# A two-layer decoder trunk: FFN features split ahead, attention values by key tile, HGRN2 scores in half columns, one fill tile moved

## The chip, the cores and the metric

One core of a Trainium2 chip runs the whole program, compiled as one launch. The metric is the device time of one execution in microseconds (us); the times of a kernel are the median of several executions.

## What is computed

The reference is a trunk of two layers over 512 tokens of 1024 features, in float32. Each layer runs a half-step SwiGLU feed-forward network (FFN), three token mixers beside each other on one normalised input, and a second FFN; every part has an RMS norm before and after.

```python
y = swiglu(rms_norm(h, ffn1_pre_g[l]), ffn1_w_gate[l], ffn1_w_up[l], ffn1_w_down[l])   # (silu(x @ gate) * (x @ up)) @ down
h = h + 0.5 * rms_norm(y, ffn1_post_g[l])
u = rms_norm(h, mix_pre_g[l]);  proj = u @ w_in[l]
y_a = rwkv7_branch(...)      # 8 heads x 64
y_b = mla_branch(...)        # 8 heads, causal softmax attention, values of 64
y_c = hgrn2_branch(...)      # 4 heads x 128, gated linear recurrence in chunks of 64
merged = gates[0] * (y_a @ rwkv_out[l]) + gates[1] * (y_b @ mla_out[l]) + gates[2] * (y_c @ hgrn_out[l])
h = h + rms_norm(merged @ w_o[l], mix_post_g[l])
# and FFN 2 like FFN 1
```

Inside a chunk of 64 tokens, HGRN2 needs the causal scores between all pairs of tokens of the chunk, each with its own product of decays. In MLA each head has softmax(q k) over the earlier keys, times its values.

## The kernel before

**Precision.** The dense products are done in three: an operand is split into a high half in the fp32r format (a cast on ScalarE, ACT, line L208) and the rest (a subtraction on VectorE, DVE, L209), and TensorE (PE) multiplies high by high, high by low and low by high (L251 to L253). Weights of 128 x 1024 or so arrive in `ws` (two buffers) through the DMA queue of SyncE (SP), and become `wh` and `wl` (three buffers each). Small products (scores, transposes) are plain float32, which PE runs in two recorded passes per instruction.

**Order of the work.** The code says which products there are; a list scheduler then lays out one queue per engine, so the order on an engine isn't that of the code. Temporary tiles `t` (seven buffers) and `m` (four), the big slots `s0` to `s10`, and the eight PSUM banks `b0` to `b7` limit how far work can be pulled ahead. The HGRN2 scores and the MLA scores take their PSUM tiles from three banks (`"a"`).

**FFN.** `gate_up` makes the inner features `hid` (22 tiles of 128 features by 512 tokens). All blocks of 256 features but the first two are done by `seven`, a seven-product scheme on half matrices; its last product ends in a SiLU (L1189) and a multiplication (L1190). `down` then multiplies the tiles of `hid` with the down weights into all eight banks. Its operand for tile j comes from the function `chunk` in `ffn`, which takes two `t` tiles, `hh` and `hl`, and splits `hid` tile j into them.

**Mixers.** `mixers` runs RWKV, then `hgrn`, then `mla`. A generator yields 41 fill tiles, projections of 24 matmuls each with 512 columns, which `pump` inserts at named places: the table `PUMP` gives how many at each (`C0` and `C1` are in `hgrn`, `B0` and `B1` in `mla`), and what is left of the 41 follows `mla`. Behind it come the output projections of the three branches.

**HGRN2 scores.** For four heads and the levels `base`, 32, 16 and 8, `hgrn` computes scores between scaled keys and queries and puts them together in `acc`. At `base`, 16 and 8 the function `scores` multiplies whole tiles of 128 x 128 tokens (L737, four per head), and a `copy_predicated` of 128 x 512 per head (L753) takes over what a mask allows; only pairs within one chunk of 64 tokens are ever taken. Level 32 has its own products of 32 x 32 (L776) and copies (L778). Behind level 8 stands `pump("C1")`, and then the keys `kx` (L783 to L785) and their transposes.

**MLA.** For each head, four row blocks: scores (L1032), row maximum, exp (L1038), scaling (L1040), transposes of the probabilities by PE (L204), a copy of them to `pT` (L1044). After each odd head the values of both heads of the pair are multiplied with `pT` into one bank, head e into partitions 64e to 64e + 63, by row block b and then key tile j (L1053, 128 columns each).

## Time and profile before

| | us |
|---|---|
| median of three runs | 2741.38 (2739.57 to 2741.49) |
| the profiled execution | 2739.44 |
| its span, first to last instruction | 2737.7 |
| PE busy | 2682.2 (98% of the span) |
| PE weight loads, beside the matmuls | 2337.6 (85%) |
| DVE busy | 1773.6 (65%) |
| ACT busy | 1348.2 (49%) |
| mean granted clock of PE | 0.994 of 2.4 GHz |

The page is read from the top: which engine is busy nearly all the time, then what that engine waited for and where, then the timeline at those places. A matmul's recorded duration includes the time it takes to run out of the array, so what a matmul costs PE is the distance from its start to the next start. A float32 matmul has two records.

### The profile page before, as it was taken

What the parts mean: (1) busy time and instruction counts of PE and PEld (TensorE: products, weight loads), DVE (VectorE), ACT (ScalarE), POOL (GpSimd) and SP (SyncE); (2) the same over time, 40 slices, a digit from 0 to 9 for tenths busy, and PEclk for the clock granted to TensorE, in tenths of its full rate; (3) what the DMA queues carried; (4) which work ended last, traced back from release to release, by engine and by line L of the source; (5) the groups of instructions that cost most, each with busy time, mean ns of one, the idle gap of its engine ahead of it and who ended that gap; (6) DMA issues with size and microseconds to landing.
All of it is one profiled execution on the core that took longest, in us unless ns stands there. A gap on an engine that the chain in (4) does not pass through costs nothing. (4 is left out here: it accounts for less than half of the span.)

```text
span 2737.7 us, 42564 instructions
## 1 busy us (share of the span) xinstructions
PE 2682.2 (98%) x17669; PEld 2337.6 (85%) x17669; DVE 1773.6 (65%) x2483; ACT 1348.2 (49%) x2133; POOL 58.7 (2%) x121
## 2 busy tenths in 40 slices
PE   8999999989999999999999999999899999999999
PEld 7998887777887889998899988877678878899987
DVE  6786357864856667784468754477558566678743
ACT  4444346346658544443344443464465585444532
POOL 0000010000000010000000000100000000100000
PEclk9999999999999999999999999999999999999999
DMA  4333332325321541333313333233253315322332
GB/s 142 110 107 123 117 123 85 112 86 173 128 86 63 172 172 62 121 105 114 123 57 98 104 127 125 99 105 101 74 204 101 106 63 180 139 93 93 116 108 77
DMA packets 223517, 307.71 MB, mean 112 GB/s; under 512 B 11856, under 2 KB 181052, under 8 KB 221788
## 3 DMA queue, kind: packets, MB, share of 16 engines
q1 hardware_dynamic: 223324, 304.99, 33.3%
q8 instruction: 139, 2.28, 0.3%
q14 instruction: 54, 0.44, 0.0%
HBM read 269.84 MB, written 35.13 MB: 111 GB/s over the span
## 5 line engine op out<-in xcount | busy, mean ns | idle before, releaser
L253 PE MATMUL b<-xhi,wl 128*128 128x256 f32 (+1 forms) x2176 | 733.5, 337 | 0.0
L251 PE MATMUL b<-xhi,wh 128*128 128x256 f32 (+1 forms) x2176 | 733.4, 337 | 0.0
L252 PE MATMUL b<-xlo,wh 128*128 128x256 f32 (+1 forms) x2176 | 732.1, 336 | 0.0
L208 ACT CAST wh<-ws 128x1024 fp32r<-128x1024 f32 (+4 forms) x448 | 393.7, 890 | 660.9 <-PE b L252 296.8
L209 DVE TENSOR_TENSOR wl<-ws,wh 128x1024 fp32r<-128x1024 f32 (+4 forms) x448 | 453.5, 1022 | 266.0 <-ACT wh L208 261.2
L251 PEld LDWEIGHTS b<-xhi,wh 128*128 128x128 f32 x2176 | 414.4, 190 | 45.1 <-issue 4.9
L253 PEld LDWEIGHTS b<-xhi,wl 128*128 128x128 f32 x2176 | 414.4, 190 | 42.0 <-issue 2.8
L252 PEld LDWEIGHTS b<-xlo,wh 128*128 128x128 f32 x2176 | 414.7, 191 | 40.6 <-issue 2.6
L251 PE MATMUL b<-s,wh 128*128 128x256 f32 (+1 forms) x1120 | 344.6, 308 | 0.0
L252 PE MATMUL b<-s,wh 128*128 128x256 f32 (+1 forms) x1120 | 344.2, 307 | 0.0
L253 PE MATMUL b<-s,wl 128*128 128x256 f32 (+1 forms) x1120 | 344.1, 307 | 0.0
L208 ACT CAST wh<-m 128x1024 fp32r<-128x1024 f32 x144 | 151.1, 1049 | 232.2 <-PE b L252 99.5
L251 PE MATMUL b<-wh,t 128*128 128x512 f32 x576 | 225.3, 391 | 8.1 <-ACT t L208 8.1
L252 PE MATMUL b<-wl,t 128*128 128x512 f32 x576 | 224.7, 390 | 0.0
L251 PEld LDWEIGHTS b<-s,wh 128*128 128x128 f32 x1120 | 213.9, 191 | 11.0 <-DVE s L994 1.2
L253 PE MATMUL b<-wh,t 128*128 128x512 f32 x576 | 223.3, 390 | 0.0
L253 PEld LDWEIGHTS b<-s,wl 128*128 128x128 f32 x1120 | 213.9, 191 | 10.0
L252 PEld LDWEIGHTS b<-s,wh 128*128 128x128 f32 x1120 | 214.0, 191 | 9.7
L209 DVE TENSOR_TENSOR wl<-m,wh 128x1024 fp32r<-128x1024 f32 x144 | 174.0, 1223 | 34.7 <-ACT wh L208 34.7
L209 DVE TENSOR_TENSOR t<-s,t 128x512 fp32r<-128x512 f32 x80 | 54.9, 691 | 166.5 <-PE b L252 150.3
L251 PEld LDWEIGHTS b<-wh,t 128*128 128x128 f32 x576 | 108.4, 188 | 31.4 <-ACT t L208 8.9
L252 PEld LDWEIGHTS b<-wl,t 128*128 128x128 f32 x576 | 108.5, 188 | 22.6
(328 smaller groups left out, 4005.6 us busy)
## 6 DMA issues: line engine op xcount, KB each, us to landing
ws<-in_w_in_dram SPq DMA_DIRECT2D x58, 1024.0 KB
ws<-in_ffn_w_up_dram SPq DMA_DIRECT2D x44, 1024.0 KB
ws<-in_ffn_w_down_dram SPq DMA_DIRECT2D x44, 1024.0 KB
ws<-in_ffn_w_gate_dram SPq DMA_DIRECT2D x43, 1024.0 KB
gd<-f SPq DMA_DIRECT2D x48, 256.0 KB
t<-gd SPq DMA_DIRECT2D x48, 256.0 KB
s<-cd SPq DMA_DIRECT2D x8, 1024.0 KB
ws<-in_w_o_dram SPq DMA_DIRECT2D x8, 1024.0 KB
```

Source lines behind the costliest of these rows:

```text
L208: self.nc.scalar.copy(hi, src)
L209: self.nc.vector.tensor_sub(lo, src, hi.bitcast(F32))
L251: nc.tensor.matmul(out, whi, xhi, start=start, stop=False, **kw)
L252: nc.tensor.matmul(out, whi, xlo, start=False, stop=False, **kw)
L253: nc.tensor.matmul(out, wlo, xhi, start=False, stop=stop, **kw)
```

## The change

Four edits.

1. *FFN.* The split of `hid` tile 0 is called in `gate_up` ahead of the last `seven`, and `down` uses that result for j = 0. `chunk` gets `hid` as an argument.
2. *HGRN2 scores.* Per token tile of 128 two products of 64 x 64 (one per chunk, u = 0 and 1, on the two column halves of the array) stand in place of one of 128 x 128; two `copy_predicated` of 64 x (4 x 64) per head stand in place of one of 128 x 512.
3. *MLA values.* The loops go by key tile j first, and each product takes all later query columns: 512, 384, 256 and 128, for both heads in turn. 8 instructions per head pair stand in place of 20.
4. *Fill.* `C1` of the table goes from 0 to 1: one fill tile of 24 matmuls comes behind the level 8 scores and no longer behind `mla`.

```diff
-    "C0": (1, 0, 1), "C1": 0, "C2": 0, "C3": 0, "B": 5, "B0": (0, 1, 0, 0), "B1": (0, 0, 0, 0, 1, 0, 0, 0),
+    "C0": (1, 0, 1), "C1": 1, "C2": 0, "C3": 0, "B": 5, "B0": (0, 1, 0, 0), "B1": (0, 0, 0, 0, 1, 0, 0, 0),
...
-        def scores(lhs, rhs, merge):
+        U = [slice(0, 64), slice(64, 128)]
+        def scores(lhs, rhs, mask):
+            mk = self.c(mask).bitcast(I32)
             for h in range(4):
-                ps = self.psum("a", (P, NT, P))
+                ps = self.psum("a", (P, NT, CH))
                 for t in range(NT):
-                    tk = slice(t * P, (t + 1) * P)
-                    nc.tensor.matmul(ps[:, t, :], lhs[:, h, tk], rhs[:, h, tk], start=True, stop=True)
-                merge(h, ps)
+                    for u in range(2):
+                        tk = slice(t * P + u * CH, t * P + u * CH + CH)
+                        nc.tensor.matmul(ps[U[u], t, :], lhs[:, h, tk], rhs[:, h, tk], start=True, stop=True)
+                for u in range(2):
+                    nc.vector.copy_predicated(acc[U[u], h, :, U[u]], mk[U[u], U[u]].unsqueeze(1).broadcast_to([CH, NT, CH]), ps[U[u]])
...
-                for b in range(NT):
-                    tk = slice(b * P, (b + 1) * P)
-                    for j in range(b + 1):
-                        for e in range(2):
-                            g = h - 1 + e
-                            nc.tensor.matmul(o[N[e], tk], vn[:, j, 64 * g:64 * g + 64], pTs[e][:, j, tk], start=j == 0, stop=j == b)
+                for j in range(NT):
+                    tk = slice(j * P, T)
+                    for e in range(2):
+                        g = h - 1 + e
+                        nc.tensor.matmul(o[N[e], tk], vn[:, j, 64 * g:64 * g + 64], pTs[e][:, j, tk], start=j == 0, stop=j == NT - 1)
...
                     A = self.token_sums()
+                if c == FF // 256 - 1:
+                    self.begun = chunk(hid, 0, -1)
                 self.seven(A, self.load(wg, KD, 256, col0=c * 256), self.load(wu, KD, 256, col0=c * 256),
...
-        self.down(NF, self.a[f"ffn{n}_w_down"][l], chunk, (0, 1, 2, 5), done)
+        self.down(NF, self.a[f"ffn{n}_w_down"][l], lambda j, n: chunk(hid, j, n) if j else self.begun, (0, 1, 2, 5), done)
```

How the queues change, at three places. In a row, `b` is a PSUM bank's tile, `s` a slot, `<-` stands between what is written and what is read, and x4 joins four alike. After the change the lines are numbered higher by 2 to 5.

PE at the boundary of the last FFN, before; `xhi`, `wl` are the last gate/up product, `t_24022` the high half of `hid` tile 0:

```order
L253 MATMUL b_3487_23790<-xhi_92,wl_23980 128x256
L251 MATMUL b_3512_24012<-wh_24026,t_24022 128x512
L252 MATMUL b_3512_24012<-wl_24027,t_24022 128x512
L251 MATMUL b_3513_24013<-wh_24026,t_24022 128x512
L252 MATMUL b_3513_24013<-wl_24027,t_24022 128x512
L251 MATMUL b_3514_24014<-wh_24026,t_24022 128x512
L252 MATMUL b_3514_24014<-wl_24027,t_24022 128x512
L251 MATMUL b_3515_24015<-wh_24026,t_24022 128x512
```

PE at the same boundary, after; `t_23809` and `t_23810` are the halves of `hid` tile 0, and L251 with `b_3515` is the first to write the bank of the last SiLU:

```order
L253 MATMUL b_3489_23818<-xhi_92,wl_24008 128x256
L251 MATMUL b_3514_24040<-wh_24050,t_23809 128x512
L252 MATMUL b_3514_24040<-wl_24051,t_23809 128x512
L253 MATMUL b_3514_24040<-wh_24050,t_23810 128x512
L251 MATMUL b_3516_24042<-wh_24050,t_23809 128x512
L252 MATMUL b_3516_24042<-wl_24051,t_23809 128x512
L253 MATMUL b_3516_24042<-wh_24050,t_23810 128x512
L251 MATMUL b_3517_24043<-wh_24050,t_23809 128x512
L251 MATMUL b_3515_24041<-wh_24050,t_23809 128x512
L252 MATMUL b_3515_24041<-wl_24051,t_23809 128x512
```

The down matmuls of the first bank read `t_24022`, cast behind the last SiLU, before, and `t_23809` after; the bank of that SiLU is first written by the eighth matmul after. ACT at this boundary, before, the SiLU (L1189) and behind it the cast of `hid` tile 0:

```order
L208 CAST wh_24026<-ws_24020 128x1024
L208 CAST wh_24058<-ws_24020 128x1024
L208 CAST wh_24092<-ws_24086 128x1024
L1189 ACTIVATE t_24007<-b_3487_23790 128x512
L208 CAST t_24022<-s_3236_21643 128x512
```

ACT after, two pieces: where the cast of `hid` tile 0 now stands, behind the SiLU of the block before, and the last SiLU (now L1194) with the cast of tile 1:

```order
L1194 ACTIVATE t_23806<-b_3460_23589 128x512
L208 CAST t_23809<-s_3236_21667 128x512
L208 CAST wh_23917<-ws_23813 128x1024
L1170 COPY t_23853<-b_3489_23818 128x512
L208 CAST wh_23947<-m_23851 128x1024
```

```order
L208 CAST wh_24050<-ws_24048 128x1024
L208 CAST wh_24082<-ws_24048 128x1024
L208 CAST wh_24116<-ws_24110 128x1024
L1194 ACTIVATE t_24035<-b_3489_23818 128x512
L208 CAST t_24078<-s_3236_21667 128x512
```

The cast moved from behind the last SiLU to 13 rows ahead of it. PE at the `base` scores of layer 0, before (L251 and L252 are fill matmuls, the L252 row the first of 23):

```order
L216 MATMUL b_931_6555<-t_6557,ones_3759 128x512
L737 MATMUL b_937_6587<-s_935_6573,s_936_6574 128x128 x4
L251 MATMUL b_944_6621<-xhi_92,wh_6617 128x512
L737 MATMUL b_938_6593<-s_935_6573,s_936_6574 128x128 x4
L737 MATMUL b_939_6599<-s_935_6573,s_936_6574 128x128 x4
L737 MATMUL b_940_6605<-s_935_6573,s_936_6574 128x128 x4
L252 MATMUL b_944_6621<-xlo_93,wh_6617 128x512
```

PE there, after (the L251 row at the end is the first of 21 fill matmuls):

```order
L216 MATMUL b_931_6555<-t_6557,ones_3759 128x512
L742 MATMUL b_937_6587<-s_935_6573,s_936_6574 64x64 x8
L251 MATMUL b_944_6641<-xhi_92,wh_6637 128x512
L252 MATMUL b_944_6641<-xlo_93,wh_6637 128x512
L253 MATMUL b_944_6641<-xhi_92,wl_6638 128x512
L742 MATMUL b_938_6598<-s_935_6573,s_936_6574 64x64 x8
L742 MATMUL b_939_6609<-s_935_6573,s_936_6574 64x64 x8
L742 MATMUL b_940_6620<-s_935_6573,s_936_6574 64x64 x8
L251 MATMUL b_944_6641<-xhi_92,wh_6637 128x512
```

Two fill matmuls moved from behind the scores of heads 1 to 3 to ahead of them. DVE there, before: merges of the four heads, other work of MLA's norms (L967), two subtractions of level 16, copies of level 32 (L778):

```order
L753 COPY_PREDICATED s_934_6571<-consts_64,b_937_6587 128x512
L753 COPY_PREDICATED s_934_6571<-consts_64,b_938_6593 128x512
L967 SCALAR_TENSOR_TENSOR m_6528<-m_6528,vt_3753,t_6539 128x512 x2
L967 SCALAR_TENSOR_TENSOR m_6529<-m_6529,vt_3753,t_6539 128x512
L967 SCALAR_TENSOR_TENSOR m_6529<-m_6529,vt_3753,t_6552 128x512
L967 SCALAR_TENSOR_TENSOR m_6530<-m_6530,vt_3753,t_6552 128x512
L753 COPY_PREDICATED s_934_6571<-consts_64,b_939_6599 128x512
L753 COPY_PREDICATED s_934_6571<-consts_64,b_940_6605 128x512
L762 TENSOR_TENSOR s_950_6693<-s_914_6502 128x64x16
L763 TENSOR_TENSOR s_950_6693<-s_914_6502 128x64x16
L778 COPY s_934_6571<-b_946_6649 32x4x32 x2
```

DVE there, after (merges L744, norms L969, subtraction L764, copies L780):

```order
L744 COPY_PREDICATED s_934_6571<-consts_64,b_937_6587 64x4x64 x2
L744 COPY_PREDICATED s_934_6571<-consts_64,b_938_6598 64x4x64
L969 SCALAR_TENSOR_TENSOR m_6528<-m_6528,vt_3753,t_6539 128x512 x2
L969 SCALAR_TENSOR_TENSOR m_6529<-m_6529,vt_3753,t_6539 128x512
L969 SCALAR_TENSOR_TENSOR m_6529<-m_6529,vt_3753,t_6552 128x512
L969 SCALAR_TENSOR_TENSOR m_6530<-m_6530,vt_3753,t_6552 128x512
L744 COPY_PREDICATED s_934_6571<-consts_64,b_938_6598 64x4x64
L744 COPY_PREDICATED s_934_6571<-consts_64,b_939_6609 64x4x64 x2
L744 COPY_PREDICATED s_934_6571<-consts_64,b_940_6620 64x4x64 x2
L764 TENSOR_TENSOR s_950_6713<-s_914_6502 128x64x16
L780 COPY s_934_6571<-b_946_6669 32x4x32 x2
```

Each merge became two, one half of head 1 stands ahead of the norms, and one of the two subtractions moved behind the copies. PE among the first MLA heads of layer 0, before; L204 are transposes of probabilities, L1032 and L1034 scores of the next head:

```order
L204 MATMUL b_1108_7629<-consts_64,t_7625 128x128 x2
L1053 MATMUL b_1115_7666<-s_1098_7597,s_1037_7206 64x128
L1053 MATMUL b_1115_7666<-s_1081_7528,s_1037_7206 64x128
L1032 MATMUL b_1124_7709<-m_7690,m_7689 128x256
L1034 LDWEIGHTS ident_656_4672
L1034 MATMUL b_1124_7709<-causal_657_4673,ident_656_4672 128x128
L1032 MATMUL b_1124_7709<-m_7690,m_7689 128x256
L1053 MATMUL b_1115_7666<-s_1098_7597,s_1037_7206 64x128
L1053 MATMUL b_1115_7666<-s_1081_7528,s_1037_7206 64x128
L204 MATMUL b_1111_7644<-consts_64,t_7640 128x128 x3
```

PE after, at the end of the first head pair (scores are L1034 and L1036):

```order
L204 MATMUL b_1119_7754<-consts_64,t_7750 128x128 x4
L1036 LDWEIGHTS ident_656_4672
L1036 MATMUL b_1135_7822<-causal_657_4673,ident_656_4672 128x128
L1034 MATMUL b_1135_7822<-m_7772,m_7771 128x512 x2
L1034 MATMUL b_1143_7848<-s_1039_7296,s_1037_7294 128x128
L1055 MATMUL b_1120_7760<-s_1103_7691,s_1041_7298 64x512
L1055 MATMUL b_1120_7760<-s_1086_7622,s_1041_7298 64x384
L1055 MATMUL b_1120_7760<-s_1103_7691,s_1041_7298 64x384
L1055 MATMUL b_1120_7760<-s_1086_7622,s_1041_7298 64x256
L1055 MATMUL b_1120_7760<-s_1103_7691,s_1041_7298 64x256
L1055 MATMUL b_1120_7760<-s_1086_7622,s_1041_7298 64x128
L1055 MATMUL b_1120_7760<-s_1103_7691,s_1041_7298 64x128
```

The value products, single pairs between transposes and scores before, stand in one group of seven behind the last transposes of the pair; an eighth (64 x 512 of the even head) stands alone 18 rows ahead of it. On PE, 43 fill matmuls follow the last value product of a layer before the change, and 11 after it; ahead of the kx transposes there are 33 more.

## Rows read from the trace of the kernel before

**Rows 1.** The page, part 1: busy us, share of the span, instructions.

```profile
PE 2682.2 (98%) x17669; PEld 2337.6 (85%) x17669; DVE 1773.6 (65%) x2483; ACT 1348.2 (49%) x2133; POOL 58.7 (2%) x121
```

**Rows 2.** PE's waits: line, what it waited for: us, times, longest.

```profile
PE b L251 <- ACT t L208: 8.1, 4, 2.0
...
PE b L737 <- ACT t L961: 2.7, 2, 1.4
```

**Rows 3.** Last FFN boundary, timeline: start, us, engine, line, tiles, count [idle <- releaser].

```profile
2609.00 0.28 PE L253 MATMUL b<-xhi,wl 128*128 128x256 f32 x1
...
2609.20 1.04 ACT L208 CAST wh<-ws 128x1024 fp32r<-128x1024 f32 x1 [1.78 <-PE b L252]
2610.16 0.59 ACT L1189 ACTIVATE t<-b 128x512 f32<-128x512 f32 x1
...
2610.64 1.13 ACT L208 CAST t<-s 128x512 fp32r<-128x512 f32 x2
...
2611.30 0.50 PE L251 MATMUL b<-wh,t 128*128 128x512 f32 x1 [2.02 <-ACT t L208]
```

**Rows 4.** Windows, first FFN boundary: length, busy by engine (PE first), PEclk, DMA.

```profile
248.00:250.00 2.00, 2.00 (x7) 1.52 (x6) 2.00 (x5) 1.96 (x4) 0.00 (x0) 0.50 0.57 231
250.00:252.00 2.00, 2.00 (x8) 1.65 (x7) 1.02 (x2) 0.22 (x1) 0.00 (x0) 0.72 0.00 0
```

**Rows 5.** Timeline of PE, layer 0, scores of levels base and 32.

```profile
729.09 2.94 PE L737 MATMUL b<-s,s 128*128 128x128 f32 x24 [1.36 <-ACT t L961]
731.79 0.47 PE L252 MATMUL b<-xlo,wh 128*128 128x512 f32 x1
...
739.13 0.45 PE L776 MATMUL b<-s 128*32 128x32 f32 x16 [0.53 <-DVE s L778]
```

**Rows 6.** Timeline of PE, RWKV part of layer 0, products of 64 columns.

```profile
607.75 0.40 PE L253 MATMUL b<-xhi,wl 128*128 128x512 f32 x1
607.98 0.39 PE L251 MATMUL b<-xhi,wh 128*128 128x512 f32 x1
608.30 0.69 PE L597 MATMUL b<-t,s 128*64 128x64 f32 x16
608.82 0.64 PE L609 MATMUL b<-s,t 128*64 128x64 f32 x16
609.38 0.50 PE L252 MATMUL b<-xlo,wh 128*128 128x512 f32 x1
```

**Rows 7.** Timeline of DVE, layer 0, merges and copies of the scores.

```profile
734.90 1.38 DVE L753 COPY_PREDICATED s<-consts,b 128x512 f32<-128x512 int32 x2
736.14 1.23 DVE L762 TENSOR_TENSOR s<-s 128x1024 f32<-128x1024 f32 x1
...
738.41 1.80 DVE L778 COPY s<-b 32x128 f32<-32x128 f32 x6
```

**Rows 8.** Window, line L1053 alone, layer 0 (PE, PEld); timeline of PE.

```profile
840.00:905.00 65.00, 14.51 (x160) 9.08 (x160) 1.00 0.22 70
...
855.86 0.66 PE L1053 MATMUL b<-s,s 128*64 128x128 f32 x8
856.44 0.66 PE L204 MATMUL b<-consts,t 128*128 128x128 f32 x4
857.03 0.44 PE L1053 MATMUL b<-s,s 128*64 128x128 f32 x4
857.40 0.68 PE L1032 MATMUL b<-m,m 128*128 128x384 f32 x2
```

**Rows 9.** A window in the heads of MLA, layer 0, all engines.

```profile
862.00:876.00 14.00, 14.00 (x106) 10.43 (x105) 11.13 (x39) 12.64 (x35) 0.00 (x0) 1.00 0.17 58
```

**Rows 10.** Timeline of DVE behind the last attention values, layer 0.

```profile
899.07 5.70 DVE L209 TENSOR_TENSOR s<-s,s 128x512 fp32r<-128x512 f32 x9 [3.20 <-PE b L1053]
```

**Rows 11.** Lines L1038 (exp), L1044 (copy): ns min/median/max, first, last start, forms.

```profile
L1038 ACT ACTIVATE t<-b,mx x64: 367/554/707, 834.2 to 2254.0; 128x128 f32<-128x128 f32 x16, 128x256 f32<-128x256 f32 x16, 128x384 f32<-128x384 f32 x16, 128x512 f32<-128x512 f32 x16
...
L1044 ACT COPY s<-b x64: 264/432/588, 842.5 to 2257.1; 128x128 f32<-128x128 f32 x16, 128x256 f32<-128x256 f32 x16, 128x384 f32<-128x384 f32 x16, 128x512 f32<-128x512 f32 x16
```

More of the change, by code (lines that the diff above doesn't have):

```diff
@@ L749, in hgrn @@
         next(norms)
-        def merge(name):
-            mk = self.c(name).bitcast(I32).unsqueeze(1).broadcast_to([P, NT, P])
-            return lambda h, ps: nc.vector.copy_predicated(acc[:, h], mk, ps)
-        scores(xk, xq, merge("base"))
+        scores(xk, xq, "base")
         for i, n in enumerate((32, 16, 8)):
@@ L768, in hgrn @@
             if n < 32:
-                scores(xs, xs, merge(f"lv{n}"))
+                scores(xs, xs, f"lv{n}")
                 continue
@@ L1067, with gate_up @@
 class Trunk(Rwkv, Hgrn, Mla, Core):
-    def gate_up(self, l, n):
+    def gate_up(self, l, n, chunk):
         nc = self.nc
@@ L1243, in ffn, with chunk @@
         nc = self.nc
-        hid = self.gate_up(l, n)
-        g = self.bcast_gain(self.a[f"ffn{n}_post_g"][l])
-        if n == 1:
-            gn = self.bcast_gain(self.a["mix_pre_g"][l])
-        elif not last:
-            gn = self.bcast_gain(self.a["ffn1_pre_g"][l + 1])
         late = []
-        def chunk(j, n):
+        def chunk(hid, j, n):
             if n < 0:
@@ L1261, in chunk @@
             return hh, hl
+        hid = self.gate_up(l, n, chunk)
+        g = self.bcast_gain(self.a[f"ffn{n}_post_g"][l])
+        if n == 1:
+            gn = self.bcast_gain(self.a["mix_pre_g"][l])
+        elif not last:
+            gn = self.bcast_gain(self.a["ffn1_pre_g"][l + 1])
         def done(t, y):
```

## Prediction

> **What bounds the kernel now.** I read the page's busy shares first, then the list of what TensorE (PE) waited for, then the timeline around each wait that the change can reach. PE is busy 98% of the span [rows 1], so time is won only by taking PE work away or closing a PE wait. Two entries of the list of waits lie where the change works [rows 2]: 8.1 us in four pieces, the start of each feed-forward (FFN) down product, and 2.7 us in two, the HGRN2 scores. The sum below is made against the profiled execution (2739.44 us) and taken off the median of the runs, 2741.38; the 1.9 us between them is part of the uncertainty.
>
> **Part 1, FFN.** At the last boundary the final gate/up matmul starts at 2609.00 and the first down matmul at 2611.30. In between ScalarE (ACT) casts a weight, applies a SiLU (L1189, from 2610.16, 0.59) and only then casts the first features, t at 2610.64, for which PE stood idle 2.02 us [rows 3]. The change puts that cast and its subtraction into the previous block, so the first down matmul waits only for weights, and the six behind it write banks that are long free. What is late next is a PSUM bank: the eighth down matmul writes the bank that the SiLU reads. It arrives at 2609.12 + 7 x 0.23 = 2610.7, the SiLU ends at 2610.75, so 0 to 0.1 us stays here; in the first FFN the tenth is gated, which is later still. Gain 2.0 each, 8.0 for four. The moved cast (0.57, half of the pair at 2610.64) goes to an engine that stands idle in every product of that block (the weight cast at 2609.20 had waited 1.78 for PE [rows 3]), its subtraction to DVE, which waits there as well, so they cost nothing; without that cover each would cost about its 0.6.
> The first boundary holds more. After its 2.0 us of idle the granted clock is 0.50 in the stretch 248 to 250, half of 2.4 GHz, and 0.72 in the next [rows 4]: (1 - 0.50) x 2 + (1 - 0.72) x 2 = 1.6 us of work lost. The other three boundaries show no such fall. PE was fully busy before the wait and nothing else differs, so without the idle I expect no fall. FFN: 9.6, bounds 2.2 (below, third rival) and 9.7.
>
> **Part 2, scores.** Before, 96 matmul records a layer of 128 columns: 24 of them take 729.09 to 731.79, 0.1125 each [rows 5], so 10.8 us. After, twice as many instructions of 64 x 64, alternately on the two column halves of the array. The nearest row is L597, the same alternation with 64 columns: 16 records from 608.30 to 608.82, 0.52 us; entering that layout costs 0.32 - 0.23 = 0.09 and leaving it 0.56 - 0.52 = 0.04 [rows 6]. Twelve heads x 0.52 + six clusters x 0.13 = 7.0, gross gain 3.8 a layer.
> These entries and exits are new here, since the old scores used the whole array like their neighbours. The Trainium skill, TensorEngine Tiling (Array Packing), section Key Properties, has it that changing the tiling mode drains TensorE; that speaks against cutting work into small clusters. The rows agree, at 0.13 us a cluster, and the sum without this price would be 0.8 us a layer better.
> Two waits change the 3.8. First, PE waits 1.36 for ACT's logarithms at 729.09 [rows 5]; that time is set by ACT and stays, but three fill matmuls stand ahead of the wait instead of one, so 2 x 0.23 = 0.46 more is done by then. Second, VectorE (DVE). At 734.90 it starts its last two merges (1.38 for two, 0.69 each), then two subtractions (736.14 to 738.41), then the copies for which PE waited until 739.13 [rows 5, 7]. After, five half merges and one subtraction stand ahead of those copies. No row shows a half merge: a copy of 128 columns takes 0.30, a merge of 512 columns 0.69 [rows 7]; 256 columns by a straight line between them are 0.43. So the copies begin at 734.90 + 5 x 0.43 + 1.13 = 738.2 and PE goes on at 738.9: 0.23 + 0.46 = 0.7 ahead of before, where its own work would have put it 1.4 ahead. The two later levels each gain 32 x 0.1125 - 4 x 0.52 - 0.26 = 1.26, as 13 to 31 fills stand between them and DVE. Sum 0.7 + 2.5 = 3.2, and 3.9 if a half merge costs 0.30; I take 3.3, so 6.6 for both layers, bounds -2.4 (second rival) and 7.9.
>
> **Part 3, attention values.** Before, 160 records a layer cost 14.5 us of PE [rows 8], which counts records while they overlap; by starts it is a little more. Eight records last 855.86 to 856.44, 0.58, and four 857.03 to 857.40, 0.37 [rows 8]. So four more records, one key tile of both heads, cost 0.21, and a cluster 0.16 besides, with the entry 0.24. The 22 clusters of a layer hold 48 such steps (40, and eight more where a head stands alone): 48 x 0.21 + 22 x 0.24 = 15.4. After there are two clusters per head pair instead of five or six: one lone matmul of 512 columns and a group of seven (512, 384, 384, 256, 256, 128, 128, the heads in turn). If the two column halves run beside each other at unequal widths as they do at equal ones, the second head's 1280 columns set the group: 10 x 0.21 + 0.24 = 2.34; the lone one costs 4 x 0.21 + 0.24 = 1.08. Four pairs x 3.42 = 13.7, with the 0.21 rounded up 14.1; I take 13.9. The group also waits for the last copy of transposed probabilities, 0.59 [rows 11], which starts when the transposes end; a few score matmuls stand between, so I put under 0.1 a pair, 0.3 a layer. Gain 15.4 - 13.9 - 0.3 = 1.2 a layer, 2.4 in all; bounds -8.0 (first rival) and 3.4.
>
> **Part 4, the fill tile.** 24 matmuls move from the end of MLA to behind the last scores; PE's work is unchanged: 0. There they cover the subtraction, exp and product that end in the kx transposes and are now queued on DVE behind eight half merges; PE, which the scores release sooner, would otherwise wait there. The price is the cover at the end: 11 fill matmuls, 2.5 us, instead of 43, 9.8 us, stand between the last attention values and the output projections. DVE's low halves begin when the last value matmul releases their slot, nine in 5.70 us [rows 10], 0.63 each; even if the first begins 1 us behind that matmul it is done at 1.6, PE wants it at 2.5 and each next one 0.7 later. 0.9 is left; the weight split has already gone by. The stores of the gate tiles and the loads of the next weights on the DMA queue come a tile earlier or later, against 24 x 0.23 = 5.5 us of slack a tile. 0, bounds 0 and -2 (a late first low half, 1 us a layer).
>
> **Sum.** 9.6 + 6.6 + 2.4 = 18.6; 2741.4 - 18.6 = **2722.8 us**, 0.7% faster.
>
> **Rivals.** First, *unequal widths don't overlap*: the 768 columns of the other head in each group then stand in line: 6 x 0.21 = 1.3 more per pair, 10.4 in all, attention loses 8.0 instead of winning 2.4: 2733.2. For it: no row has two widths side by side. Against: four more records cost 0.21 [rows 8], where four of the full array take 4 x 0.1125 = 0.45 [rows 5], so each half goes on by itself.
> Second, *the merges bound the scores*: a half merge costs as much as a whole one, 0.69. Then the copies at level 32 come at 734.90 + 3.45 + 1.13 = 739.5, 1.1 later than before, and the eight merges of each later level take 5.5 us of DVE between scores: I walk to 1.2 lost per layer instead of 3.3 won, 2731.8. Against: the 0.30 copy [rows 7]. The Trainium skill states this rule in TensorEngine Tiling (Array Packing), section PSUM Bottleneck: tiling speeds up the matmuls but not the reading out of PSUM. No run here shows yet which it is.
> Third, *the split ahead doesn't reach PE*: some bank or slot holds the first down matmul until the SiLU's end at 2610.75. Then each boundary wins 2611.30 - 2610.75 = 0.55, 2.2 in all, perhaps with the clock fall left: 2730.2. Against: in the new order the bank of that SiLU comes eighth.
> Fourth, the slow side, *a softmax chain laid open*: the old small value clusters stood in PE's row between scores and transposes, and so bridged the way through exp, transposes and copy, 0.71 + 0.66 + 0.59 = 2.0 us for the widest block [rows 8, 11] (its scaling apart). With values gathered in one group the bridge goes. Open once in each of 16 heads that is 32 us: 2741.4 - 16.2 + 32 = 2757. It decides the sign from (16.2 + 5.5) / 16 = 1.4 us a head. For it: ACT is busy 12.64 of 14 us there [rows 9], so it has little to give. Against: eight more fills now stand between the heads, 1.8 us a layer, and PE was busy 14.00 of 14.00 us there [rows 9].
>
> **How the numbers follow.** A measurement here can tell about 0.2%, 5.5 us, from no change, so "faster" is below 2735.9. Forecast 0.60, first rival 0.13, second 0.09, third 0.07, fourth 0.04; 0.07 for partial losses that add up to within 0.2% (new short waits, a clock fall somewhere else). Faster 0.88, same 0.07, slower 0.05. All upper bounds together give 2741.4 - 9.7 - 7.9 - 3.4 = 2720, less the 1.9 by which single executions differ, 2718; the first rival with its spread gives 2734. The range 2718 to 2734 leaves out some 0.15.
>
> **What would show it.** After the change: the entry "L251 <- ACT t" of four times 2.0 gone from PE's list of waits, and clock 1.00 throughout 246 to 254; score records of about 32 ns and half merges near 0.43; the copies behind the fills still waited for by PE for about 1 us a layer; the group of seven lasting 2.4 us (3.7 if the first rival holds); no wait of PE at the kx transposes or at the first output projection; PE idle within MLA under 1 us a layer (fourth rival if above 10). A PE that waits in MLA would break the forecast most.

## The result

| | before | after |
|---|---|---|
| median, us | 2742.94 (2739.29 to 2746.99, 12 runs) | 2726.2 (2724.63 to 2736.5, 12 runs) |
| ratio | | 0.9947, 95% interval 0.9935 to 0.9959 |
| profiled execution, us | 2739.44 | 2736.01 |

The change makes the kernel 0.5% faster: by the ratio 14.5 us (11 to 18), by the medians of the runs made together 16.7. The forecast was 2722.8, with a range from 2718 to 2734. The profiled execution of after is 10 us above its own median, because for 25 us in RWKV of layer 0 its granted clock was at the lower level (shown at the end; only kernels with the split ahead show it); so the two profiles are compared by stretches and not by their spans.

The page of after, part 1, against [rows 1]: PE still has 98%, and VectorE (DVE) has 6 us more work.

```profile
PE 2683.8 (98%) x17669; PEld 2331.5 (85%) x17669; DVE 1779.8 (65%) x2507; ACT 1347.4 (49%) x2133; POOL 58.5 (2%) x121
```

PE's waits in after, those that the change touches, against [rows 2] (us, times, longest):

```profile
PE b L742 <- ACT t L963: 2.0, 2, 1.0
...
PE b L778 <- DVE s L744: 1.8, 4, 0.5
...
PE b L251 <- DVE s L996: 1.3, 2, 0.7
PE b L778 <- DVE s L780: 1.1, 2, 0.6
...
PE b L742 <- DVE s L768: 0.5, 2, 0.3
PE b L204 <- DVE s L787: 0.4, 2, 0.2
```

The entry of 8.1 us at the FFN boundaries is gone. New are small entries that name DVE: half merges (L744), products of the scores and of kx (L768, L787), and a product in MLA's query projections (L996) that the change does not touch. The one of 1.1 us at level 32 (L780) was there before.

**The FFN boundary in after**, against [rows 3]: timeline of PE, then of ACT, at the last FFN.

```profile
2607.71 0.28 PE L253 MATMUL b<-xhi,wl 128*128 128x256 f32 x1
2607.83 0.40 PE L251 MATMUL b<-wh,t 128*128 128x512 f32 x1
```

```profile
2588.75 0.59 ACT L1194 ACTIVATE t<-b 128x512 f32<-128x512 f32 x1
2589.24 0.61 ACT L208 CAST t<-s 128x512 fp32r<-128x512 f32 x1
...
2607.91 1.05 ACT L208 CAST wh<-ws 128x1024 fp32r<-128x1024 f32 x1 [1.77 <-PE b L252]
```

The cast of `hid` tile 0 is at 2589.24, 18 us ahead of the boundary, and the first down matmul starts 0.12 us behind the last gate/up matmul (before 2.30). At the first boundary the clock stays up, where [rows 4] has 0.50 and 0.72. Windows of after (length, busy by engine with PE first, granted clock, DMA):

```profile
248.00:250.00 2.00, 2.00 (x10) 1.65 (x10) 2.00 (x5) 1.63 (x4) 0.00 (x0) 1.00 0.97 399
250.00:252.00 2.00, 2.00 (x11) 1.65 (x10) 1.85 (x3) 1.02 (x2) 0.00 (x0) 1.00 0.03 8
```

**The scores in after**, against [rows 5]: PE in layer 0, levels base, 32 and 16.

```profile
734.76 0.69 PE L742 MATMUL b<-s,s 128*64 128x64 f32 x16
...
737.32 1.73 PE L742 MATMUL b<-s,s 128*64 128x64 f32 x48 [0.98 <-ACT t L963]
...
744.81 0.45 PE L778 MATMUL b<-s 128*32 128x32 f32 x16 [0.40 <-DVE s L744]
...
745.75 0.45 PE L778 MATMUL b<-s 128*32 128x32 f32 x16 [0.50 <-DVE s L744]
...
747.64 0.45 PE L778 MATMUL b<-s 128*32 128x32 f32 x16 [0.55 <-DVE s L780]
```

```profile
754.95 0.39 PE L251 MATMUL b<-xhi,wh 128*128 128x512 f32 x1
755.26 1.62 PE L742 MATMUL b<-s 128*64 128x64 f32 x48
756.81 0.50 PE L252 MATMUL b<-xlo,wh 128*128 128x512 f32 x1
757.31 0.69 PE L742 MATMUL b<-s 128*64 128x64 f32 x16
757.93 0.50 PE L253 MATMUL b<-xhi,wl 128*128 128x512 f32 x1
758.26 0.39 PE L251 MATMUL b<-xhi,wh 128*128 128x512 f32 x1
```

48 records from 755.26 to 756.81 are 0.52 for 16, as [rows 6] gave it. But a fill matmul costs PE 0.23 in a row of its kind, 0.31 on the way in (754.95 to 755.26), 0.33 on the way out (757.93 to 758.26), and one alone between two clusters costs 0.50 (756.81 to 757.31). The 0.31 and the 0.33 are not new: around whole-array scores of before, the last fill ahead takes 0.31 (748.21 to 748.52) and the first behind 0.31 (749.44 to 749.75), though those scores use the whole array like the fills. PE of before, level 16:

```profile
748.21 0.39 PE L251 MATMUL b<-xhi,wh 128*128 128x512 f32 x1
748.52 1.16 PE L737 MATMUL b<-s 128*128 128x128 f32 x8
749.44 0.47 PE L252 MATMUL b<-xlo,wh 128*128 128x512 f32 x1
749.75 0.39 PE L253 MATMUL b<-xhi,wl 128*128 128x512 f32 x1
```

And at level 32 PE now stops three times for DVE, 1.45 us in all, where [rows 5] has one stop of 0.53.

DVE beside it, against [rows 7]:

```profile
743.25 2.35 DVE L744 COPY_PREDICATED s<-consts,b 64x256 f32<-64x256 int32 x5
745.64 1.23 DVE L764 TENSOR_TENSOR s<-s 128x1024 f32<-128x1024 f32 x1
746.89 2.40 DVE L780 COPY s<-b 32x128 f32<-32x128 f32 x8
...
756.25 3.78 DVE L744 COPY_PREDICATED s<-consts,b 64x256 f32<-64x256 int32 x8
```

Five half merges take 2.35 and eight 3.78: 0.47 each, where a whole one took 0.69. 24 halves a layer are 11.3 us of DVE where 12 wholes were 8.3.

**The attention values in after**, against [rows 8]: the end of the first head pair on PE.

```profile
864.36 1.07 PE L1055 MATMUL b<-s,s 128*64 128x512 f32 x2
865.37 0.44 PE L204 MATMUL b<-consts,t 128*128 128x128 f32 x2
...
868.97 2.37 PE L1055 MATMUL b<-s,s 128*64 128x512 f32 x14
871.26 0.33 PE L204 MATMUL b<-consts,t 128*128 128x128 f32 x1
```

The lone matmul of 512 columns costs 1.01 us, the group of seven 2.29, with no wait ahead of either.

**Where the time went, by stretches.** A stretch starts at a named matmul of PE. The scores' stretch runs from the first score matmul to the first kx transpose, the kx stretch from there to the first MLA score, the MLA stretch from there to the first output projection. From the length of each I take 0.227 us for each fill matmul in it, as fills move between stretches. "Edge" is the stretch from the output projections to the first down matmul of the second FFN. Layer 0, in us, with layer 1 within 0.3 of it where the clock was up:

| kernel | scores | kx | MLA | edge, less before |
|---|---|---|---|---|
| before | 15.15 | 41.4 | 55.1 | 0 |
| after | 13.61 | 41.8 | 52.9 | -2.2 |
| scores alone | 17.74 | 42.9 | 55.0 | 0 |
| values alone | 15.12 | 41.4 | 52.8 | 0 |
| fill alone | 14.74 | 42.5 | 55.4 | 0 |
| FFN alone | 15.15 | 41.4 | 55.1 | -2.2 |
| all but the scores | 14.76 | 42.4 | 52.8 | -2.2 |
| two heads a bank | 12.13 | 44.3 | 52.9 | -2.2 |

Per layer, after wins 1.5 in the scores, 2.2 in MLA, 2.2 at each of two FFN boundaries, and gives back 0.4 in the kx stretch: 2 x (1.5 + 2.2 + 4.4 - 0.4) = 15.4, and 1.7 for the clock at the first boundary: 17.1 us, beside 16.7 by the medians and 14.5 by the ratio. The 1.7 holds for that boundary alone; what the clock does elsewhere comes further down.

### The profile page after: what moved, and what is told of

It is laid out like the page before. It is cut to its first block, busy times and chain, and to the rows that moved or that the text cites. A ratio compares the mean times of both kernels' runs of the same rounds, so it can differ in the third digit from the quotient of the medians.

```text
span 2734.2 us, 42594 instructions
## 1 busy us (share of the span) xinstructions
PE 2683.8 (98%) x17669; PEld 2331.5 (85%) x17669; DVE 1779.8 (65%) x2507; ACT 1347.4 (49%) x2133; POOL 58.5 (2%) x121
## 5 line engine op out<-in xcount | busy, mean ns | idle before, releaser
L251 PE MATMUL b<-xhi,wh 128*128 128x256 f32 (+1 forms) x2176 | 734.9, 338 | 0.0
L252 PE MATMUL b<-xlo,wh 128*128 128x256 f32 (+1 forms) x2176 | 734.2, 337 | 0.0
L208 ACT CAST wh<-ws 128x1024 fp32r<-128x1024 f32 (+5 forms) x448 | 393.1, 889 | 649.7 <-PE b L252 273.5
L209 DVE TENSOR_TENSOR wl<-ws,wh 128x1024 fp32r<-128x1024 f32 (+5 forms) x448 | 453.1, 1022 | 258.9 <-ACT wh L208 255.6
L251 PEld LDWEIGHTS b<-xhi,wh 128*128 128x128 f32 x2176 | 415.3, 191 | 45.4 <-issue 4.4
L252 PEld LDWEIGHTS b<-xlo,wh 128*128 128x128 f32 x2176 | 415.3, 191 | 41.5 <-issue 3.2
L253 PEld LDWEIGHTS b<-xhi,wl 128*128 128x128 f32 x2176 | 415.2, 191 | 41.2 <-issue 1.9
L251 PE MATMUL b<-s,wh 128*128 128x256 f32 (+1 forms) x1120 | 344.4, 307 | 1.3 <-DVE s L996 1.3
L252 PE MATMUL b<-s,wh 128*128 128x256 f32 (+1 forms) x1120 | 344.1, 307 | 0.0
L251 PE MATMUL b<-wh,t 128*128 128x512 f32 x576 | 224.2, 389 | 0.0
L252 PE MATMUL b<-wl,t 128*128 128x512 f32 x576 | 224.1, 389 | 0.0
L251 PEld LDWEIGHTS b<-s,wh 128*128 128x128 f32 x1120 | 213.9, 191 | 11.9 <-DVE s L996 2.2
L252 PEld LDWEIGHTS b<-s,wh 128*128 128x128 f32 x1120 | 213.9, 191 | 9.8
L209 DVE TENSOR_TENSOR wl<-m,wh 128x1024 fp32r<-128x1024 f32 x144 | 174.0, 1224 | 33.3 <-ACT wh L208 33.3
L209 DVE TENSOR_TENSOR t<-s,t 128x512 fp32r<-128x512 f32 x80 | 55.0, 691 | 158.6 <-PE b L252 154.2
L251 PEld LDWEIGHTS b<-wh,t 128*128 128x128 f32 x576 | 108.1, 188 | 23.1 <-ACT t L1194 0.6
L253 PEld LDWEIGHTS b<-wh,t 128*128 128x128 f32 x576 | 108.1, 188 | 22.4
```

Of the source, the lines that this page charges most:

```text
L208: self.nc.scalar.copy(hi, src)
L209: self.nc.vector.tensor_sub(lo, src, hi.bitcast(F32))
L251: nc.tensor.matmul(out, whi, xhi, start=start, stop=False, **kw)
L252: nc.tensor.matmul(out, whi, xlo, start=False, stop=False, **kw)
L253: nc.tensor.matmul(out, wlo, xhi, start=False, stop=stop, **kw)
```

## The experiments

The theory was the prediction's: three independent gains and a fill that costs nothing. The rival that the trace of after raised: the three mixer edits hang together through DVE, and each part alone is worth something else than in the sum. The first four runs make one part of the change alone, in the kernel before.

**FFN alone.** The kernel before, with this and the `chunk` that goes with it:

```diff
+                if c == FF // 256 - 1:
+                    self.begun = chunk(hid, 0, -1)
```

> Only the first part: the split of the first inner features ahead of the last gate and up products. Theory A (each boundary gives 2.1 to 2.3 us, the first one 3.9 with the clock fall that it no longer causes, as the trace after shows): 10.5 us off the kernel before in undisturbed executions, so about 2729, and no wait of PE for the cast in the list of waits. Rival B (a boundary gives 2.0 and the clock fall only moves elsewhere): 8 us off, 2731. Rival C (the bank of the last SiLU holds PE): 2 us off.

Measured: 2732.13 us, before beside it 2744.67, ratio 0.997 (0.9956 to 0.9983). Each boundary is 2.2 us shorter, and no other stretch moves by more than 0.1 where the clock was the same. This part stands on its own. By the ratio it is 8.2 us faster (4.7 to 12.1), which does not tell the first theory's 10.5 from rival B's 8. B's fall elsewhere is seen: in this profile the granted clock is 0.50 for 25 us in RWKV of layer 0, where before has 1.00.

**Scores alone.**

```diff
+                        nc.tensor.matmul(ps[U[u], t, :], lhs[:, h, tk], rhs[:, h, tk], start=True, stop=True)
+                for u in range(2):
+                    nc.vector.copy_predicated(acc[U[u], h, :, U[u]], mk[U[u], U[u]].unsqueeze(1).broadcast_to([CH, NT, CH]), ps[U[u]])
```

> Only the scores in half columns, without the fill tile behind them. Theory A (the trace after: about 0.3 us per cluster for the change of the tiling, and merges of 0.47 start to start, leave 1.7 us a layer; and the kx transposes wait when the fill tile is missing): the scores give 3.5, the missing cover takes 2 to 4 us a layer back at the line of the transposes (L204 waiting for DVE), so 0 to 4 us slower than before. Rival B (the prices of the forecast, cover not needed): 6.6 us faster. Rival C (the scores gain 3.5 and the cover is not needed): 3.5 faster.

Measured: 2750.57 us, ratio 1.0027 (1.0018 to 1.0037): slower, by 4.0 us a layer in the stretches, 8 in all, more than the first theory's 0 to 4. PE's waits show where:

```profile
PE b L204 <- DVE s L787: 7.6, 2, 3.8
```

Without the fill tile, PE reaches the kx transposes 3.8 us ahead of DVE's product L787. DVE in layer 0 of this kernel, from the last merges on:

```profile
753.18 2.28 DVE L785 TENSOR_TENSOR s<-s 128x2048 f32<-128x2048 f32 x1
755.50 3.76 DVE L744 COPY_PREDICATED s<-consts,b 64x256 f32<-64x256 int32 x8
759.29 2.29 DVE L787 TENSOR_TENSOR s<-s,s 128x2048 f32<-128x2048 f32 x1
```

The eight half merges of level 8 stand in DVE's queue right ahead of the product, back to back. Not all of the 4.0 is the wait itself: in both layers the granted clock is at the lower level for 3.4 us behind it (0.51 over the 3 us shown), which takes 1.7 us in the kx stretch:

```profile
762.00:765.00 3.00, 3.00 (x16) 2.97 (x14) 3.00 (x3) 1.62 (x3) 0.00 (x0) 0.51 0.03 5
```

The work of PE alone did get shorter: the stretch less its fills, its waits of 3.27 and the last wait of 3.80 is 17.74 - 3.27 - 3.80 = 10.67, where before has 15.15 - 1.89 = 13.26.

**Values alone.**

```diff
+                for j in range(NT):
+                    tk = slice(j * P, T)
+                    for e in range(2):
```

> Only the attention values by key tile. Theory A (the group of seven takes 2.3 us and the lone one 1.0, as the trace after shows, against 15.4 us a layer before): 1.5 us a layer, 3 us faster. Rival B (part of it returns as waits for the transposed probabilities, or ACT is late in MLA): 0 to 1 faster, with new waits of PE for L1044 of over 0.5 us a layer.

Measured: 2739.0 us, ratio 0.9985 (0.9976 to 0.9995); the MLA stretch is 2.3 us shorter in each layer, the others equal. By the ratio it is 4.1 us, more than the first theory's 3, and no wait of PE for the copies (L1044) appears. This part stands on its own too.

**Fill alone.**

```diff
-    "C0": (1, 0, 1), "C1": 0,
+    "C0": (1, 0, 1), "C1": 1,
```

> Only the fill tile moved behind the last scores. Theory A (the fill is neutral as long as the scores are slow): within 1 us of before, no new wait at the output projections. Rival B (the cover at the end of MLA is needed): 2 to 5 us slower, with PE waiting for DVE halves (L209) at the first output projection.

Measured: 2744.59 us, ratio 1.0004 (0.9995 to 1.0013); by stretches 1.1 to 1.3 us a layer longer, which the time can't tell from none. Neither theory holds by the stretches: the fill is not neutral, and the wait is not at the output projections. PE's waits have a new entry, at MLA's query projections (L994 is here the line that is L996 in after):

```profile
PE b L251 <- DVE s L994: 2.0, 2, 1.1
```

The four parts alone come to 0.997, 1.0027, 0.9985 and 1.0004: in sum 0.14% faster, where all four together are 0.53% faster. The difference, 0.39% or 10.7 us by the ratios (each known to 0.1%) and 12.6 us by the stretches, lies in the scores and the fill: FFN and values gain the same alone and together (2.2 a boundary, 2.2 to 2.3 a layer in MLA), while the scores and the fill, each a loss alone by the stretches, win 1.1 us a layer together.

**After again**, the changed kernel a second time beside the single parts, to have a profile at full clock:

> The changed kernel as it is, for the comparison on the same chip and a second trace. Theory A: 2724 to 2726 where the clock does not fall in the RWKV part, 2731 to 2737 where it does (the trace after shows a granted clock of 0.50 from 516 to 541, 11.5 us); part by part the same distances as in the first trace: feed-forward boundaries 10.5 us, HGRN2 and MLA stretch 3.3 a layer.

Measured: 2725.59 us, ratio 0.9942 (0.9923 to 0.996); its stretches are those of after but for 1.3 us in the scores of layer 0, where the granted clock fell behind the wait for the logarithms (0.91 over 720 to 740).

**All but the scores**: after with the whole scores and merges of before put back.

```diff
-                        nc.tensor.matmul(ps[U[u], t, :], lhs[:, h, tk], rhs[:, h, tk], start=True, stop=True)
+                    nc.tensor.matmul(ps[:, t, :], lhs[:, h, tk], rhs[:, h, tk], start=True, stop=True)
```

> The changed kernel with the old whole-tile scores and merges; the other three parts stay. Theory A (scores and fill tile are worth something only together, 1.7 us a layer by the trace): 3 to 4 us slower than the changed kernel, and the fill tile alone buys nothing. Rival B (the half columns bring nothing, the gain of the stretch is all from the attention values): equal to the changed kernel within 1 us.

Measured: 2729.4 us, ratio 0.994 (0.9925 to 0.9955). Between this kernel and after the scores are worth 1.7 to 1.9 us a layer by stretches, about half of the 3.3 predicted; alone they cost 4.0. This is what the first theory expected. The medians, 3.8 us apart, agree; the ratios do not tell the two kernels apart, as two of the eight executions of after again were 10 us or more longer than the rest.

**Two heads a bank.** If the many half merges cap the gain, then merging two heads in one instruction (64 x 512, one cluster a level instead of two, four merges a level and not eight) should give it back.

```diff
+            for p in range(2):
+                ps = self.psum("a", (P, 2 * NT, CH))
+                for i in range(2 * NT):
+                    h, t = 2 * p + i // NT, i % NT
```

> The changed kernel, but two heads' scores share a PSUM bank, so a merge takes 64 x 512 and a level is one cluster instead of two with a lone fill matmul between. Theory A (the scores lost their gain to entering and leaving the half-column layout, 0.3 us per cluster and 0.27 more for a lone fill between two, and to the count of merges): three clusters fewer per layer save 1.4, merges of 0.7 for two heads instead of 4 x 0.47 shorten VectorE by 1 us a level and so the waits at level 32 by 1 us: 4 to 5 us faster than the changed kernel. Rival B (only VectorE counts): 2 us faster, with the clusters' distance unchanged. Rival C (a merge costs by its columns, two heads at once are no cheaper): 2.5 us faster from the clusters alone.

Measured: 2725.88 us, ratio 0.9933 (0.9918 to 0.9949), which the time does not tell from after; by stretches it is 1.0 to 1.2 us a layer longer. None of the three expectations, all of 2 us faster or more, came. The scores' stretch is 1.5 us a layer shorter, as expected, and the kx stretch 2.5 longer. Its waits:

```profile
PE b L251 <- DVE s L997: 2.9, 4, 1.0
...
PE b L779 <- DVE s L781: 2.0, 2, 1.0
...
PE b L823 <- DVE s L811: 1.3, 2, 0.7
PE b L204 <- DVE s L788: 1.2, 2, 0.6
```

The query projections (L997), the state updates (L811) and the kx product (L788) each hold PE longer than in after: most of what PE saves in the scores it waits for behind them (in the kx stretch of layer 0 it waits 3.1 us, in after 1.2).

**Level 32 in one bank too**: two copies there and not eight, so DVE has less to do still.

```diff
+            ps = self.psum("a", (P, 4 * NT, 32))
+            for i in range(4 * NT):
+                h, t = i // NT, i % NT
```

> As the kernel with two heads a bank, and level 32 too: its four heads fill one bank, two copies of 32 x 512 instead of eight of 32 x 128, one cluster instead of two. Theory A: the wait of PE for the copies (0.55 a layer) and two changes of layout go, 1 us of VectorE too: 2 us faster than the kernel with two heads a bank, 6 to 7 faster than the changed kernel. Rival B (VectorE is no longer awaited there): 0.6 us faster, by the cluster alone.

Measured: 2737.66 us (2724.68 to 2751.47), ratio 0.9969 (0.9946 to 0.9993). The runs scatter with the granted clock, so I read it by stretches: scores 11.2, 1.0 shorter than with two heads a bank; kx stretch of layer 0 45.25, 0.9 longer. The expectation of 6 to 7 us is missed, and that of rival B too, as the two stretches together are no shorter than with two heads a bank. The wait at level 32 (L781) is gone, and in its place PE waits elsewhere, for a copy on ACT (new) and for the state updates on DVE (1.3 before):

```profile
PE b L743 <- ACT f L263: 2.7, 2, 1.3
PE b L823 <- DVE s L811: 2.7, 2, 1.4
```

Cutting DVE's work in the scores gave PE nothing, since PE then meets the next late step.

**One more fill tile ahead of the query projections**, in after and in two heads a bank; and, in two heads a bank, at a third place, among the HGRN2 state products (C2). If that wait is a lack of cover, a tile there should win it.

```diff
-"B0": (0, 1, 0, 0)
+"B0": (1, 1, 0, 0)
```

> After with one more fill tile (24 matmuls) ahead of MLA's first query projections, B0 = (1, 1, 0, 0), taken from what follows MLA. Theory A (the 1.3 us in two that PE waits for the query products of VectorE are a lack of cover, the rest of what the change opened): that wait goes, and the time falls by 0.7 to 1.3 us against after (2724 to 2726 where after gives about 2726). Theory B (VectorE is late all the way from the score merges, so a tile only shifts where PE waits): the wait moves to the MLA scores or to the output projections, which lose their last cover, and the time is the same or up to 2 us longer.

Measured: 2727.66 us, ratio 0.9943 (0.9928 to 0.9959). By stretches it is 1.1 us a layer slower than after: the kx stretch wins 0.6 (41.2), the rest loses 1.7. The entry L251 <- L996 is gone, and two others are new, at the output projections and in the MLA heads:

```profile
PE b L252 <- DVE s L209: 1.7, 2, 0.8
...
PE b L1055 <- ACT s L1046: 0.8, 2, 0.4
```

The second theory holds here: the wait moved. L252 <- L209 is the late low half that the prediction priced at 1 us a layer as its bound for part 4; it appears one fill tile later than the change goes.

> Two heads per PSUM bank (four merges a level and not eight), with the same fill tile ahead of the query projections. Two heads a bank alone made the score stretch 1.5 us a layer shorter and the stretch from kx to MLA 2.6 longer. Theory A: the tile covers the 1.45 us a layer of waiting at the query projections; the stretch from kx to MLA falls by 1 to 1.5 us a layer net of its fill, and the time is 2 to 3 us below that of two heads a bank alone. Theory B: the waits move behind the tile, and the time is within 1 us of it.

Measured: 2726.18 us, ratio 0.9943 (0.9928 to 0.9958). By stretches 0.4 to 0.8 us a layer better than two heads a bank, between what the two theories gave: the query wait closes, and the two entries just shown appear, with the same 1.7 and 0.8.

```diff
-"C2": 0
+"C2": (1, 0, 0, 0, 0, 0, 0, 0)
```

> Two heads per PSUM bank, with one fill tile more among the HGRN2 state products, C2 = (1, 0, 0, 0, 0, 0, 0, 0). Theory A (what is missing is cover right behind the kx transposes, where PE waits 0.66 us for the state updates of VectorE): that wait goes, 0.7 us a layer. Theory B: the waits at the query projections stay as they are (1.45 us a layer) since they come from VectorE later; the time is within 1.5 us of two heads a bank alone.

Measured: 2727.58 us, ratio 0.9942 (0.9926 to 0.9958). By stretches 0 to 0.3 us a layer better than two heads a bank. The wait for L811 falls from 1.3 to 0.6, that at the query projections goes as well, which the second theory did not expect, and the output projections wait instead (again 1.7). None of the three beats after.

## Why the prediction was right, and where it was not

The time came in the range, 3.4 us above the forecast. That the sum is close is in part luck: two terms were too small and one too large, and they nearly cancel:

| term | predicted | measured by stretches |
|---|---|---|
| FFN, 4 boundaries and the clock | 9.6 | 4 x 2.2 + 1.7 = 10.5 |
| scores (and what they do to the kx stretch) | 6.6 | 2 x (1.5 - 0.4) = 2.2 |
| attention values | 2.4 | 2 x 2.2 = 4.4 |
| sum | 18.6 | 17.1 |

**FFN: the wait right and a little small, the clock not won for sure.** The wait goes to 0.12 us, and nothing is late behind it, as the bank of the last SiLU is eighth. The gain is 2.2 and not 2.0, since the distance from matmul to matmul was 2.30 and is 0.12, and the wait alone was taken. The clock fall was priced at 1.6 and is 1.7 in the first boundary. Over all runs it is a matter of chance: in the profiles of the four kernels that keep the wait (before, scores, values and fill alone) the granted clock over the 20 us from the boundary is 0.91 at 7 of 16 boundaries, and in the nine that have the split ahead it is 1.00 at all 36. At the boundaries that is 1.7 x 7/16 x 4 = 3.0 us an execution on average. The prediction was right that no fall comes there, but it took the 1.6 as won for the whole execution, and that no run shows: with the split ahead the clock falls in another place (last section), and the mean granted clock is 0.991 in the nine profiles, 0.993 in the four. What stands is 4 x 2.2 = 8.8 us.

**Scores: right in direction, the step on VectorE failed.** The gross gain on PE was put at 3.8 a layer and is 13.26 - 10.67 = 2.6. The term that was mis-sized is the change of layout: 0.13 a cluster, taken at one entry and one exit in [rows 6]. What is left to explain by the runs is (10.8 - 2.6 - 6.24) / 6 = 0.33 a cluster. Added up by the starts in layer 0, with waits taken off, the score matmuls went from 10.6 to 6.6 us (6.24 was taken, but 16 of them take 0.61 up to the fill behind), the fills around them from 1.4 to 2.3 above 0.227 each, and level 32 with what follows from 1.3 to 1.8. The two lone fills are 0.6 of the 2.3. The matmul at 609.38 in [rows 6] is such a lone one, between clusters of L609 and L581; it takes 0.44 to the next start, and was there to be read:

```profile
609.82 0.68 PE L581 MATMUL b<-t,s 64*64 64x64 f32 x16
```

The prediction's reason fails as well: it called the entries and exits new, but the whole-array scores of before have them, at 0.31 each. The Trainium skill, TensorEngine Tiling (Array Packing), section Key Properties, says that a change of the tiling mode drains TensorE. How much of the 0.33 is such a drain no run here tells, since the fills beside whole-array scores start as late.

The half merge, 0.43 by a straight line, is 0.47. At level 32 the prediction had PE go on 0.7 early instead of 1.4; its waits grew from 0.53 to 1.45, by 0.9 where 0.7 was taken. But for the later levels it said that 13 to 31 fills stand between the scores and DVE, and took the whole gain. It had read what PE waited for, not how full DVE was. One window would have told: the scores of layer 0 from the last merges of base to the kx transposes, first before, then after (DVE is third of the engines):

```profile
735.00:759.00 24.00, 23.47 (x193) 19.78 (x192) 23.79 (x28) 12.46 (x11) 0.00 (x0) 1.00 0.09 35
```

```profile
743.00:773.00 30.00, 28.14 (x284) 21.96 (x282) 29.15 (x44) 13.62 (x14) 0.00 (x0) 1.00 0.15 48
```

DVE was busy 23.79 of 24 us in before already; PE waited for it only 0.53, having about as much to do itself. Over its scores the change takes 2.6 us from PE and gives DVE 24 x 0.47 - 12 x 0.69 = 3.0 more, so DVE sets the end of the stretch (scores alone shows it: DVE works without a gap from 732 us on, up to L787, for which PE waits 3.8), and PE needs the fill tile to have something to do.

**Part 4: the sum of 0 is wrong as a separate term.** The prediction said that the fill covers the kx product, and this holds (0.4 us of wait in two, where 7.6 are without it). But it is not free: the fill alone costs 1.1 to 1.3 us a layer, scores alone 4.0, and both beside the other parts win 1.1. Nor is it work for PE alone: fills bring weight splits to DVE. In after three of them stand among the last merges and ahead of the kx product, where DVE has no gap; scores alone has none there:

```profile
761.20 1.22 DVE L209 TENSOR_TENSOR wl<-ws,wh 128x1024 fp32r<-128x1024 f32 x1
...
768.39 2.35 DVE L209 TENSOR_TENSOR wl<-ws,wh 128x1024 fp32r<-128x1024 f32 x2
```

What the tile buys and what the scores win can't be booked apart. The cost was looked for at the output projections; in after they start without a wait, and it is at the query projections (L996, 1.3 us in two), which the prediction did not name.

**Attention: right, and twice as large.** The group of seven was put at 2.34 and takes 2.29, the lone one at 1.08 and takes 1.01: 4 x 3.30 = 13.2 a layer, where 13.9 was taken. The 0.3 for the last copy did not come: the scores of the next heads stand between. That is 0.7 + 0.3 of the 1.0 that was missed.

**The rivals.** Unequal widths do overlap: the group takes 2.29 where the first rival had 2.34 + 1.3 = 3.6. The half merge is nearer the straight line than the whole price (0.47 between 0.43 and 0.69), so the second rival's price fails; its mechanism, that the merges on DVE bound the scores, is what scores alone shows. The rule of the Trainium skill that stood beside it (TensorEngine Tiling (Array Packing), section PSUM Bottleneck), that tiling speeds up the matmuls but not the reading out of PSUM, fits in that the merges went up from 8.3 to 11.3 us a layer while the score matmuls went down; but DVE was full before the tiling as well, and 21 half merges are only 9.9 of its 29.15 us. The split ahead reaches PE, so the third fails. The fourth, the open softmax chain, does not show: the MLA stretch has 0.06 us of idle, and the window of [rows 9], taken from after, has PE busy throughout, with ACT at 11.58 (it lies 17 us behind the first MLA score here and 30 in [rows 9], so the heads differ):

```profile
862.00:876.00 14.00, 14.00 (x85) 10.15 (x84) 12.03 (x45) 11.58 (x34) 0.00 (x0) 1.00 0.12 39
```

## What to carry to other kernels

Before an edit that shortens one engine's work, read the busy time of the others in that very stretch, not only who waited for whom: an engine busy 23.8 of 24 us that hardly anyone waits for is the next bound. Cover is a stock that moves: each fill tile put in front of one wait opened another, so edits that use the same fills or the same busy engine are to be priced together, and tested together as well as alone. The price of a change of layout on PE is read at the start of the second matmul behind it, not the first, and against the same place beside whole-array products. A clock fall that goes with a wait may come back elsewhere, so the granted clock is compared over whole executions, several of them.

## What was not expected of the hardware

*The clock without an idle PE.* In the profiled execution of after, the granted clock is 0.50 (the lower level, 1.2 GHz) for 25 us in RWKV of layer 0, while PE's records fill the stretch; in after again the same stretch runs at 1.00. Window 516 to 541 of the first, then of the second:

```profile
516.00:541.00 25.00, 25.00 (x90) 19.34 (x91) 11.10 (x18) 4.45 (x8) 2.85 (x3) 0.50 0.01 1
```

```profile
516.00:541.00 25.00, 25.00 (x144) 19.77 (x145) 14.13 (x21) 10.83 (x22) 2.85 (x3) 1.00 0.18 55
```

Ahead of it PE had waited 0.63 us at 513.06 in the one and 0.75 at 512.65 in the other, on the same line (L481), so the wait does not tell the two apart. FFN alone shows the same fall at the same place (0.50), level 32 in one bank too (0.51), and two heads a bank half of it (0.74). All four have the split ahead; the profiles of the four kernels that keep the wait have 1.00 there. The times say the same: with the split ahead, 15 of 66 executions lie over 9 us above the shortest of their kernel (6 of them of level 32 in one bank, which has a second long fall, in layer 1); without it, none of 103. The fall costs some 11 us, as much as a good edit here. So it goes with the split ahead, which takes the falls of 1.7 us at the boundaries away; what sets it off stays open.

*The clock behind a wait.* A wait of 2.0 us at an FFN boundary was followed by a fall at 7 of 16 places, in kernels whose PE queues agree there for 60 matmuls on either side; what decides is open too.

*A lone matmul between two clusters on the column halves* costs 0.50 us and not 0.23; there are two in a layer. Two heads a bank, which has none of them and three clusters fewer, has 1.5 us a layer less in the scores.
